# First frames' squares behind all their splits, first weights in two pieces, and the post-norm's g applied in the copy out of PSUM, in a two-layer streaming encoder

## The chip, the cores and the metric

The kernel runs on one core of one Trainium2 chip, as one launch. The metric is the device time of a launch in microseconds (us), the median of several runs. One launch of each kernel is also taken apart by the hardware profiler; its rows are what the text reads. TensorE is the matrix engine (PE in the rows, its weight loads PEld), VectorE is DVE, ScalarE is ACT, GpSimd is POOL, and SyncE (SP) issues all of the kernel's DMA transfers, in its own order. Matmul results land in PSUM, everything else lives in SBUF.

## The reference

Two layers run over 1056 frames of 1024 channels: 1024 frames of a new stream (the prompt) and 32 of a running one (the sample, with key and value caches). Each layer is a sandwich-normalised mixer:

```python
h = RMSNorm(x) * g_pre
au, av, az, bq, bk, bv, bz, cq, ck, cv, cz = split(h @ w_in)    # 1024 x 3072
ya = gMLP(au, norm(av)) * silu(az)           # mixing over chunks of 128 frames, 256 wide
yb = window_attention(bq, bk, bv, t5 bias, sinks) * silu(bz)    # own chunk of 64 + 2 before, 512 wide
yc = band_attention(cq, ck, cv, clipped bias) * silu(cz)        # own chunk + 8 before, 256 wide
y = concat(ya, yb, yc) @ w_out               # 1024 x 1024
x = x + RMSNorm(y) * g_post
```

The outputs are x of the prompt and the sample after the second layer, and the keys, values and normalised av rows that a later step would need. RMSNorm(y) is y times one number per frame, R = (mean of y squared + 1e-6) to the power -0.5; g is one number per channel.

## The kernel before

**Tiling.** Activations lie with channels on partitions: 8 k-chunks of 128 channels by 1056 frames. The frames form three tiles t0, t1, t2 of 384, 384 and 288 columns (the sample is the end of t2). `Y` holds the frames or the layer's values, `R` the factor per frame. Each operand of a dense matmul is split into a high and a low half: for activations `hh` and `hl` (with g_pre multiplied in), for weights `whi` and `wlo` (made from `wraw`, the tile as loaded, 128 x 512, four k-chunks). One k-step is three matmuls (hh by whi, hl by whi, hh by wlo). A dense block, 128 output channels by one frame tile, is 8 k-steps, so 24 matmuls, into one PSUM bank. A layer has 24 input blocks by 3 tiles (names bk bv bq0 ... cz1; letter a, b, c for the mixer) and 8 output blocks by 3 tiles. The weights of a few blocks are kept in the tiles named kk, vv, ph, pl rather than whi, wlo; the rows show these names.

**The norm before the matmul.** The first layer's blocks start before R is known, since R scales a whole frame: matmuls run on Y * g, and R is multiplied in when a block is copied out (`v<-S,R`, `v<-d,R`, `Y<-d,R`). R of a tile needs squares of its eight k-chunks (ScalarE), summed into a tile `v` (`v<-v,tmp`, VectorE or GpSimd), summed over partitions by TensorE (`pt<-ones,v`), turned into `r` (VectorE, then the power -0.5 on GpSimd with `mhalf`), and spread to all partitions by TensorE again (`pt<-ident,r`) and a ScalarE copy (`R<-pt`).

**What sets the order.** The program is written by a greedy planner while it is built. `Clock` (line 91) estimates when each engine is free. Work other than dense matmuls is put as steps into lanes (`lane(name).put(fn, ok, at, mark, ...)`): `ok` says which marks must be done, `at` when its operands are there. Before each k-step `pump` (line 1147) takes the steps that are ready. `two` (line 402) gives a two-input operation to VectorE or GpSimd, whichever ends it earlier by the estimate, and `copy` (line 415) picks ScalarE or VectorE. `split` (line 429) makes the high and the low half. So a change of one step shifts later choices all over the program. All instructions are recorded in one helper, which is why nearly all rows carry line L291; they are told apart by tile names.

**Buffers and tables.** PSUM has three banks named d, two named S (also used for scores), two pt and one pv. The order of the input blocks after the first three comes from the table `ORDERS`; the first three (bk, bv, bq0) run for t0 and t1 first, into d and S banks. SBUF tag "wraw" has 3 buffers, "v" 4, "tmp" 3.

**The places that the change touches.** `load`, `halve` and `split_at` (lines 499 to 540) load and split the weights. `square` (line 1203) does one chunk's square and its sum, and waits for the mark `0.X{t}.{k}`, chunk k's own split. `boundary` (line 1264) closes a layer for a tile: per chunk Y * g * R, plus the residual x, a store, and for the next layer the new split. The copy out of an output block is in the dense loop (line 1395); only the last tile of the last layer applies g there. `layer_consts` (line 1074) fills tables for the relative bias of mixer c.

Of the kernel before, what the change touches and what calls it, by code (L numbers as in the profile page):

```python
# [37 lines left out]
BLOCKS = "bk bv bq0 bq1 bq2 bq3 av0 av1 ck0 ck1 cv0 cv1 cq0 cq1 au0 au1 az0 az1 bz0 bz1 bz2 bz3 cz0 cz1".split()  # L38

ORDERS = (  # L40
    "bk bv bq0 bq2 bq1 bq3 av1 cq0 cv0 ck0 av0 bz2 cq1 cv1 au0 ck1 bz1 au1 az0 az1 bz3 bz0 cz1 cz0".split(),
    "bk bv bq0 bq1 bq2 av0 ck1 cv0 bq3 bz2 bz0 av1 ck0 cq0 cq1 bz1 cv1 au1 au0 bz3 az0 az1 cz0 cz1".split(),
)

FIRST = {"b": 0, "c": 4, "a": 6}
# [261 lines left out]
def encoder(  # L307
# [87 lines left out]
    def tmp():  # L395
        return tl([128, 384], "tmp")
# [46 lines left out]
    def lane(name):  # L443
        return lanes.setdefault(name, Lane())
# [42 lines left out]
    def take_spare(l, a="kk"):  # L487

        if l not in spare:
            x = tl([128, 2048], a, F32R)  # L490
            held[x.tensor.name] = 4
            spare[l] = [x[:, 512 * i : 512 * i + 512] for i in range(4)]

    for x in weights:
        kind, l, n = x[:3]
        for g in (0, 1):
            h = (x, g)

            def load(h=h, g=g, src=w[l, BLOCKS.index(n)] if kind == "w" else wo[l, n]):
                raw[h] = tl([128, 4, 128], "wraw")  # L500
                dma.dma_start(raw[h], src[:, 4 * g : 4 * g + 4, :])

            place = PLACES[2 * BLOCKS.index(n) + g] if kind == "w" and n in BLOCKS[:START] else None
            if kind == "o":
                place = KEPT.get((n, x[3]))

            def where(kind=kind, l=l, place=place, x=x):

                if kind == "o" and place:
                    return place if x in spare or {f"{l}.c1", f"{l}.SC"} <= done and free(place) else None  # L510
                if place == "kk":
                    return "kk" if l in spare or l == 0 or {f"{l - 1}.c1", f"{l - 1}.SC"} <= done and free("kk", 2) else None
                if place == "ph":
                    return "ph" if (l == 0 or f"{l - 1}.c1" in done) and free("ph") else None
                if free("whi"):
                    return "whi"
                return "ph" if kind == "o" and f"{l}.c1" in done and free("ph") else None

            def halve(h=h, l=l, n=n, kind=kind, where=where, x=x):
                a = where()  # L520
                if a in ("kk", "vv"):
                    to = l if kind == "w" else x
                    take_spare(to, a)
                    hi, lo = (spare[to].pop() for _ in (0, 1))
                else:
                    hi, lo = (tl([128, 512], c, F32R) for c in (a, {"whi": "wlo", "ph": "pl"}[a]))
                whi[h], wlo[h] = (x.rearrange("p (k c) -> p k c", k=4) for x in (hi, lo))
                split(whi[h], wlo[h], raw[h])
                let_go(raw.pop(h))

            def split_at(h=h, l=l, where=where, to=l if kind == "w" else x):
                a = where()
                t = after("act", [raw[h]])
                if a in ("kk", "vv"):
# [538 lines left out]

    def layer_consts(l):

        box = {}

        def mix():
            dma.dma_start(wt, aws[l])

            for g in range(4):
                pool.affine_select(wt[:, g, :], wt[:, g, :], pattern=[[1, 128]], compare_op=ALU.is_ge, fill=0.0,
                                   base=0, channel_multiplier=-1)

        def mix_bias(g):
            half = g % 2
            dma.dma_start(bsb[64 * half : 64 * half + 64, g // 2, :], abias[l, g : g + 1, :].to_broadcast([64, 128]))

        def sample_sink(j, g):
            dma.dma_start(ssk[32 * g : 32 * g + 32, j : j + 1],  # L1090
                          sinks[l : l + 1, 4 * j + g : 4 * j + g + 1].to_broadcast([32, 1]))
            if (j, g) == (1, 3):
                pool.tensor_scalar(ssk[:, 2:4], ssk[:, 0:2], -1.0, None, op0=ALU.mult)

        def table():
            c, e = box["c"], box["e"] = tmp(), tmp()
            dma.dma_start(c[:4, 0:256], crel[l, :, 1:257])
            pool.tensor_copy(c[:4, 256:384], c[:4, 255:256].to_broadcast([4, 128]))
            pool.tensor_copy(e[:4, :], c[:4, 255:256].to_broadcast([4, 384]))
            lane("store").put(lambda: dma.dma_start(fc_d[l][:, 0:384], c[:4, :]), None, lambda: after("dma", [c[:4, :]]))  # L1100
            lane("store").put(lambda: dma.dma_start(fc_d[l][:, 384:FC_W], e[:4, : FC_W - 384]), None,
                              lambda: after("dma", [e[:4, :]]), f"{l}.LC")

        return ([table, mix, lambda: dma.dma_start(gab, ag[l : l + 1, :].to_broadcast([128, 256]))]
                + [lambda g=g: mix_bias(g) for g in range(4)] + [lambda j=j, g=g: sample_sink(j, g) for j in (0, 1) for g in range(4)])

# [67 lines left out]
    def first_layer():  # L1174
# [20 lines left out]
        for t in range(3):  # L1195
            a, T = TOK[t]
            box = {}
            for k in range(KB):
# [6 lines left out]
                        box["sq"] = sq_tile(t)  # L1205
                    sq_add(box["sq"], Y[:, k, a : a + T], T, k == 0)

                lane(f"sq{t}").put(square, lambda k=k, ok=marks(f"0.X{t}.{k}"): ok() and (k or free("v")), lambda x_at=x_at: max(x_at(), clock.t["act"] - FIRST_AHEAD[3]), f"0.Q{t}.{k}")
            rms_steps(lane(f"bnd{t}"), box, t, marks(f"0.Q{t}.7"), f"0.R{t}")

    chunks = {}
# [55 lines left out]
    def boundary(l, t, box):  # L1267
# [7 lines left out]
        for k in range(8):  # L1275
            y = Y[:, k, a : a + T]

            def x(k=k, y=y):
                g = g_sb[:, l, 1, k : k + 1]
                dve.scalar_tensor_tensor(y, y, g, R[:, a : a + T], op0=ALU.mult, op1=ALU.mult)  # L1280
                c = chunk.pop(k)
                two(y, y, c[:, :T], ALU.add)
                let_go(c)
# [14 lines left out]
    def layer_steps(l):  # L1298
        units = [Unit(l, br, i, q) for br, n in (("b", 4), ("c", 2)) for i in range(n) for q in range(8 // NQ[br])]
        over = marks("0.R0") if l == 0 else marks(*(f"{l - 1}.{x}" for x in ("b3", "c1", "A", "SB", "SC")))  # L1300
        lane("lc").put(lambda: sink_consts(l), over, None, f"{l}.LS")
        for f in layer_consts(l):
            lane("lc").put(f, marks(f"{l}.b1.bias"), lambda: clock.t["dma"])
# [16 lines left out]
    for e, (x, t) in enumerate(plan):  # L1320
# [21 lines left out]
        for k in range(KB):  # L1342
            h = (x, k // 4)

            def at():
                if k == 0 and bank() is None or h not in whi or f"{l}.{'X' if kind == 'w' else 'ys'}{t}.{k}" not in done:
                    return None
                ops = [whi[h], wlo[h], hh[t][:, k, :], hl[t][:, k, :]]
                return max(after("pe", ops), slot(bank(), "pe") if k == 0 else 0.0)

            pump(at)
# [29 lines left out]
        else:  # L1381
# [123 lines left out]
```

## Time and profile before

| | us |
|---|---|
| median of three runs | 1014.42 |
| lowest, highest of them | 1014.22, 1015.7 |
| the profiled execution | 1014.88 |
| its span, first to last instruction | 1013.2 |
| TensorE, VectorE, ScalarE, GpSimd busy | 996.8, 762.9, 511.6, 69.5 |
| mean granted clock of TensorE | 0.998 |

The 1.7 us between the profiled execution's time and its span lie around the instructions. A busy share says how full an engine is; matmuls are pipelined, so a matmul's own duration (0.34 us at 384 columns) is about twice the distance from one start to the next in a full run. In a timeline a row shows its start, its duration, the engine and the operation with output and inputs, and in brackets the idle time before it and what ended that. The granted clock is 1.00 at full speed.

### The profile page before, as it was taken

How to read it: one execution, taken by the hardware profiler on the slowest of the kernel's cores; microseconds unless marked ns; L12 is line 12 of the kernel's file. 1: busy time of each engine (PE TensorE's matmuls, PEld its weight loads, DVE VectorE, ACT ScalarE, POOL GpSimd, SP SyncE). 2: the span in 40 equal slices, each digit the busy share in tenths (PEclk: the TensorE clock that was granted, in tenths of full speed). 3: DMA queues.
4: the chain of work that ended last, by engine and by line, in shares of the span. 5: the costliest groups of instructions: out<-in, count | busy, mean ns of one | idle time of the engine just before them, and what ended most of it. 6: DMA issues, size and time to landing. Idle time of an engine off the chain costs nothing.

```text
span 1013.2 us, 18902 instructions
## 1 busy us (share of the span) xinstructions
PE 996.8 (98%) x6630; PEld 969.2 (96%) x6630; DVE 762.9 (75%) x1973; ACT 511.6 (50%) x1304; POOL 69.5 (7%) x150
## 2 busy tenths in 40 slices
PE   8999999999999999999999999999999999999997
PEld 7999999989999999999999999999899999999996
DVE  8778778877777775858897789877687787577654
ACT  7555566554444443745643566645454444356332
POOL 0100000001100000000111000000200000000121
PEclk9999999999999999999999999999999999999999
DMA  8232313212123011446543322231122212126633
GB/s 267 68 79 79 84 50 88 64 48 57 58 66 96 22 43 63 145 126 187 153 137 114 79 66 78 59 85 35 52 67 64 65 43 75 42 76 196 188 109 128
DMA packets 83343, 91.26 MB, mean 90 GB/s; under 512 B 13232, under 2 KB 59696, under 8 KB 83248
## 3 DMA queue, kind: packets, MB, share of 16 engines
q1 hardware_dynamic: 83248, 90.05, 30.2%
q8 instruction: 52, 0.85, 0.4%
q14 instruction: 43, 0.35, 0.1%
HBM read 66.11 MB, written 11.31 MB: 76 GB/s over the span
## 4 chain that ended last, share of the span: by engine, by line
PE 82%; DVE 8%; DMA 3%; ACT 3%; issue 2%; SPq 1%; POOL 1%; DVEq 0%; ACTq 0%; POOLq 0%
PE d L291 54%; PE S L291 14%; PE pt L291 8%; PE pv L291 6%; DVE Y L291 3%; DVE s L291 1%; ACT tmp L291 1%; DVE wlo L291 1%; DVE pl L291 1%; DVE v L291 1%; SPq L291 1%; DMA wraw<-in_wo_dram 1%; DVE hl L291 1%; DMA wraw<-in_w_dram 1%; DMA bias<-fb_d 1%
## 5 line engine op out<-in xcount | busy, mean ns | idle before, releaser
L291 PE MATMUL d<-hh,whi 128*128 128x384 f32 (+1 forms) x1144 | 378.6, 331 | 0.0
L291 PE MATMUL d<-hh,wlo 128*128 128x384 f32 (+1 forms) x1144 | 369.7, 323 | 0.5 <-DVE wlo L291 0.4
L291 PE MATMUL d<-hl,whi 128*128 128x384 f32 (+1 forms) x1144 | 369.0, 323 | 0.0
L291 PEld LDWEIGHTS d<-hh,whi 128*128 128x128 f32 x1144 | 215.5, 188 | 2.2 <-issue 1.7
L291 PEld LDWEIGHTS d<-hh,wlo 128*128 128x128 f32 x1144 | 215.0, 188 | 1.3 <-DVE wlo L291 1.1
L291 PEld LDWEIGHTS d<-hl,whi 128*128 128x128 f32 x1144 | 215.7, 189 | 0.3
L291 ACT ACTIVATE s<-s,nm 128x256 f32<-128x256 f32 (+5 forms) x196 | 108.5, 554 | 150.0 <-DVE nm L291 149.8
L291 DVE TENSOR_TENSOR pl<-pt,ph 128x512 fp32r<-128x512 f32 (+2 forms) x136 | 80.6, 623 | 26.2 <-ACT ph L291 25.9
L291 DVE TENSOR_TENSOR wlo<-wraw,whi 128x512 fp32r<-128x512 f32 x116 | 80.2, 693 | 14.3 <-ACT whi L291 11.0
L291 ACT ACTIVATE ph<-pt 128x512 fp32r<-128x512 f32 (+2 forms) x136 | 69.0, 542 | 25.8 <-PE pt L291 24.7
L291 DVE TENSOR_TENSOR Y<-pv,tmp 64x256 f32<-64x256 f32 x96 | 40.4, 421 | 44.2 <-ACT tmp L291 43.2
L291 PE MATMUL pv<-pl,vv 128*128 128x256 f32 (+1 forms) x288 | 71.1, 286 | 0.6 <-DVE pl L291 0.3
L291 PE MATMUL pv<-ph,vv 128*128 128x256 f32 (+1 forms) x288 | 70.0, 269 | 0.2 <-ACT ph L291 0.2
L291 PE MATMUL pt<-ident,s 128*128 128x128 f32 x488 | 68.6, 274 | 0.0
L291 ACT ACTIVATE whi<-wraw 128x512 fp32r<-128x512 f32 x94 | 58.7, 624 | 18.5 <-DMA wraw<-in_wo_dram 13.7
L291 PE MATMUL S<-kk,qh 128*128 128x256 f32 (+3 forms) x224 | 66.1, 313 | 1.2 <-DVE nm L291 1.2
L291 PE MATMUL S<-kk,ql 128*128 128x256 f32 (+3 forms) x224 | 62.1, 295 | 0.0
L291 ACT ACTIVATE tmp<-tmp 128x384 f32<-128x384 f32 (+1 forms) x48 | 23.8, 496 | 68.1 <-DVE tmp L291 68.1
L291 PEld LDWEIGHTS pt<-ident,s 128*128 128x128 f32 x488 | 56.0, 140 | 2.2 <-DVE s L291 0.5
L291 PEld LDWEIGHTS pv<-pl,vv 128*128 128x128 f32 x288 | 54.4, 189 | 3.1 <-DVE pl L291 2.4
L291 DVE CUSTOM_DVE_ANT_0 s<-S,bias,nsink 128x256 f32<-128x256 f32 (+1 forms) x128 | 54.3, 463 | 2.8 <-POOL bias L291 1.5
L291 ACT ACTIVATE tmp<-pv 64x256 f32<-64x256 f32 x96 | 36.4, 379 | 39.2 <-DVE Y L291 20.4
(183 smaller groups left out, 1765.8 us busy)
## 6 DMA issues: line engine op xcount, KB each, us to landing
wraw<-in_w_dram SPq DMA_DIRECT2D x96, 256.0 KB, 2.9
wraw<-in_wo_dram SPq DMA_DIRECT2D x72, 256.0 KB, 3.0
qr<-Y SPq DMA_DIRECT2D x384, 32.0 KB, 1.9
x_d<-Y SPq DMA_DIRECT2D x16, 192.0 KB, 3.2
out_y_dram<-Y SPq DMA_DIRECT2D x16, 192.0 KB, 2.8
Y<-in_xT_dram SPq DMA_DIRECT2D x5, 576.0 KB, 4.8
bias<-fc_d SPq DMA_DIRECT2D x8, 320.0 KB, 3.8
bias<-fb_d SPq DMA_DIRECT2D x16, 128.0 KB, 3.1
```

The lines of the kernel that those rows point to most:

```text
L291: return f(*args, **kw)
```

## The change

Four edits. (1) The first weight tile is loaded in two transfers of 256 columns, and split in two pieces; a dense k-step may start with the first piece. (2) The `square` steps of t0 wait for the split of t0's last chunk, not of their own. (3) g of the post-norm is always applied in the copy out of PSUM; the boundary then multiplies by R only, by `two`, so on VectorE or GpSimd. The squares for the norm are still taken from PSUM, before g. (4) The two tables in `layer_consts` use tag "v" instead of "tmp". Beside them both tables `ORDERS` change: the first lines show one of them.

```diff
@@ ORDERS, one of its two lines
-    "bk bv bq0 bq2 bq1 bq3 av1 cq0 cv0 ck0 av0 bz2 cq1 cv1 au0 ck1 bz1 au1 az0 az1 bz3 bz0 cz1 cz0".split(),
+    "bk bv bq0 bq1 bq2 av1 bq3 cq0 cv0 ck0 av0 cq1 cv1 bz1 bz2 ck1 au1 az0 au0 az1 bz0 bz3 cz1 cz0".split(),
@@ -491,6 +491,15 @@
+    begin = (weights[0], 0)
+    ready = set()
+
+    def rest():
+
+        ready.add(begin)
+        split(whi[begin][:, 2:4, :], wlo[begin][:, 2:4, :], raw[begin][:, 2:4, :])
+        let_go(raw.pop(begin))
+
@@ -498,7 +507,9 @@
                 raw[h] = tl([128, 4, 128], "wraw")
-                dma.dma_start(raw[h], src[:, 4 * g : 4 * g + 4, :])
+                for k in (0, 2) if h == begin else (0,):
+                    m = 2 if h == begin else 4
+                    dma.dma_start(raw[h][:, k : k + m, :], src[:, 4 * g + k : 4 * g + k + m, :])
@@ -525,12 +536,17 @@
+                if h == begin:
+                    split(whi[h][:, 0:2, :], wlo[h][:, 0:2, :], raw[h][:, 0:2, :])
+                    lane("wsplit").steps.appendleft((rest, None, lambda: after("act", [raw[begin][:, 2:4, :]]), None, False, ()))
+                    return
+                ready.add(h)
                 split(whi[h], wlo[h], raw[h])
                 let_go(raw.pop(h))
...
@@ -1093,13 +1108,14 @@
-            c, e = box["c"], box["e"] = tmp(), tmp()
+            c, e = tl([128, 384], "v"), tl([128, 384], "v")
...
@@ -1205,7 +1221,7 @@
-                lane(f"sq{t}").put(square, lambda k=k, ok=marks(f"0.X{t}.{k}"): ok() and (k or free("v")), lambda x_at=x_at: max(x_at(), clock.t["act"] - FIRST_AHEAD[3]), f"0.Q{t}.{k}")
+                lane(f"sq{t}").put(square, lambda k=k, ok=marks(f"0.X{t}.{k if t else KB - 1}"): ok() and (k or free("v")), lambda x_at=x_at: max(x_at(), clock.t["act"] - FIRST_AHEAD[3]), f"0.Q{t}.{k}")
@@ -1277,7 +1293,7 @@
                 g = g_sb[:, l, 1, k : k + 1]
-                dve.scalar_tensor_tensor(y, y, g, R[:, a : a + T], op0=ALU.mult, op1=ALU.mult)
+                two(y, y, R[:, a : a + T], ALU.mult)
                 c = chunk.pop(k)
                 two(y, y, c[:, :T], ALU.add)
@@ -1343,9 +1359,9 @@
-                if k == 0 and bank() is None or h not in whi or f"{l}.{'X' if kind == 'w' else 'ys'}{t}.{k}" not in done:
+                if k == 0 and bank() is None or h not in whi or k % 4 > 1 and h not in ready or f"{l}.{'X' if kind == 'w' else 'ys'}{t}.{k}" not in done:
@@ -1392,7 +1408,7 @@
-            copy(Y[:, n, a : a + T], d[:, :T], g_sb[:, l, 1, n : n + 1] if end else None)
+            copy(Y[:, n, a : a + T], d[:, :T], g_sb[:, l, 1, n : n + 1])
```

The start of VectorE's program, as a piece of the difference between the two orders; hl_71 and hh_68 are the halves of t0, v_128 is the sum of its squares, wlo the weights' low halves (a row with x3 stands for three in a row):

```order
-L291 CAST whi_130<-wraw_93 128x512
-L291 TENSOR_TENSOR wlo_131<-wraw_93,whi_130 128x512
+L291 TENSOR_TENSOR wlo_130<-wraw_93,whi_129 128x256 x2
 L291 TENSOR_SCALAR hh_68<-Y,g_sb 128x384
-L291 SCALAR_TENSOR_TENSOR hl_71<-Y,g_sb,hh_68 128x384 x2
-L291 TENSOR_TENSOR v_128<-v_128,tmp_145 128x384
-L291 TENSOR_TENSOR v_128<-v_128,tmp_148 128x384
-L291 SCALAR_TENSOR_TENSOR hl_71<-Y,g_sb,hh_68 128x384 x2
-L291 TENSOR_TENSOR wlo_162<-wraw_97,whi_161 128x512
-L291 TENSOR_TENSOR v_128<-v_128,tmp_165 128x384
-L291 TENSOR_TENSOR v_128<-v_128,tmp_168 128x384
+L291 SCALAR_TENSOR_TENSOR hl_71<-Y,g_sb,hh_68 128x384 x4
```

Four square sums stood between the low halves of t0; now four low halves follow one another, and the first weight's high half is no longer made on VectorE.

Later on VectorE, before the first copy out of a block (S_141 before, S_138 now: block bk of t0). Before:

```order
L291 SCALAR_TENSOR_TENSOR hl_72<-Y,g_sb,hh_69 128x384 x3
L291 TENSOR_TENSOR v_259<-v_259,tmp_292 128x384
L291 SCALAR_TENSOR_TENSOR hl_73<-Y,g_sb,hh_70 128x288
L291 TENSOR_TENSOR v_259<-v_259,tmp_300 128x384
L291 TENSOR_TENSOR v_259<-v_259,tmp_306 128x384
L291 TENSOR_TENSOR v_259<-v_259,tmp_312 128x384
L291 SCALAR_TENSOR_TENSOR hl_73<-Y,g_sb,hh_70 128x288
L291 TENSOR_TENSOR v_325<-S_141,R 128x384
L291 CAST kk_124<-v_325 64x384
```

And after, where v_192 sums the squares of t0, v_327 those of t1, v_385 those of t2, and r_364 is r of t0:

```order
L291 TENSOR_TENSOR v_192<-v_192,tmp_324 128x384
L291 TENSOR_TENSOR v_327<-v_327,tmp_332 128x384
L291 TENSOR_TENSOR v_327<-v_327,tmp_338 128x384
L291 TENSOR_TENSOR v_327<-v_327,tmp_344 128x384
L291 TENSOR_TENSOR v_327<-v_327,tmp_357 128x384
L291 TENSOR_SCALAR r_364<-pt_360 128x3
L291 TENSOR_TENSOR v_327<-v_327,tmp_367 128x384
L291 TENSOR_TENSOR v_327<-v_327,tmp_373 128x384
L291 TENSOR_TENSOR v_327<-v_327,tmp_379 128x384
L291 TENSOR_TENSOR v_385<-v_385,tmp_391 128x288
L291 TENSOR_TENSOR v_385<-v_385,tmp_394 128x288
L291 TENSOR_TENSOR v_405<-S_138,R 128x384
```

The last sum of t0 and the r made from it now stand behind all the low halves of t0, t1 and t2 (hl_73), and the copy out behind the sums of two tiles.

The boundary of tile t1 in the last layer, on VectorE. Before:

```order
L291 SCALAR_TENSOR_TENSOR Y<-Y,g_sb,R 128x384
L291 TENSOR_TENSOR Y<-Y,s_12223 128x384
L291 SCALAR_TENSOR_TENSOR Y<-Y,g_sb,R 128x384
L291 TENSOR_TENSOR Y<-Y,s_12234 128x384
L291 SCALAR_TENSOR_TENSOR Y<-Y,g_sb,R 128x384
L291 TENSOR_TENSOR Y<-Y,bias_12249 128x384
L291 SCALAR_TENSOR_TENSOR Y<-Y,g_sb,R 128x384
L291 TENSOR_TENSOR Y<-Y,bias_12269 128x384
L291 SCALAR_TENSOR_TENSOR Y<-Y,g_sb,R 128x384
L291 TENSOR_TENSOR Y<-Y,bias_12285 128x384
L291 TENSOR_TENSOR wlo_12581<-wraw_12367,whi_12580 128x512
L291 TENSOR_TENSOR v_12475<-v_12475,tmp_12618 128x288
```

After, on VectorE:

```order
L291 TENSOR_TENSOR Y<-Y,R 128x384
L291 TENSOR_TENSOR Y<-Y,s_12182 128x384
L291 TENSOR_TENSOR Y<-Y,s_12193 128x384
L291 TENSOR_TENSOR Y<-Y,s_12217 128x384
L291 TENSOR_TENSOR Y<-Y,s_12226 128x384
L291 TENSOR_TENSOR Y<-Y,s_12237 128x384
L291 TENSOR_TENSOR Y<-Y,R 128x384
L291 TENSOR_TENSOR Y<-Y,bias_12246 128x384
L291 TENSOR_TENSOR Y<-Y,bias_12266 128x384
L291 TENSOR_TENSOR Y<-Y,R 128x384
L291 TENSOR_TENSOR Y<-Y,bias_12281 128x384
L291 TENSOR_TENSOR wlo_12583<-wraw_12370,whi_12582 128x512
```

And after, on GpSimd, where before no Y row stood:

```order
L291 TENSOR_TENSOR r_12463<-r_12463,mhalf 128x3
L291 MEMSET v_12478 128x96
L291 TENSOR_TENSOR Y<-Y,R 128x384 x4
L291 TENSOR_TENSOR v_12478<-v_12478,tmp_12525 128x288
L291 TENSOR_TENSOR Y<-Y,R 128x384
L291 TENSOR_TENSOR pl_12556<-wraw_12358,ph_12555 128x512
L291 TENSOR_TENSOR v_12478<-v_12478,tmp_12573 128x288
```

Three of the eight multiplies by R stay on VectorE and five stand on GpSimd, among the square sums of t2 and a weight's low half (pl).

VectorE in the second layer, around a copy out (v from d) and the first scores of mixer b (ISA rows: scores plus bias). Before:

```order
L291 SCALAR_TENSOR_TENSOR Y<-Y,g_sb,R 128x288
L291 TENSOR_TENSOR Y<-Y,bias_6523 128x288
L291 TENSOR_TENSOR ql_6809<-qr_6728,qh_6808 128x256
L291 ISA s_6812,nm_6813<-S_6815,bias_6784,nsink 128x128
L291 ISA nm_6813 128x1
L291 ISA s_6812,nm_6813<-S_6815,bias_6784,nsink 128x128
L291 ISA nm_6813 128x1
L291 TENSOR_TENSOR v_6827<-d_6762,R 128x384
L291 TENSOR_SCALAR hh_70<-Y,g_sb 128x288
```

After:

```order
L291 TENSOR_TENSOR Y<-Y,R 128x288
L291 TENSOR_TENSOR Y<-Y,bias_6525 128x288
L291 TENSOR_TENSOR ql_6806<-qr_6734,qh_6805 128x256
L291 TENSOR_TENSOR ql_6822<-qr_6739,qh_6821 128x256
L291 TENSOR_TENSOR v_6829<-d_6795,R 128x384
L291 SCALAR_TENSOR_TENSOR hl_73<-Y,g_sb,hh_70 128x288
L291 TENSOR_TENSOR v_6636<-v_6636,tmp_6833 128x288
L291 ISA s_6847,nm_6848<-S_6850,bias_6758,nsink 128x128
L291 ISA nm_6848 128x1
```

The copy out of d stood behind the score rows, and now stands ahead of them.

## Rows read from the trace of the kernel before

**Rows 1.** The page's first part: busy us, share of the span, instructions.
```profile
PE 996.8 (98%) x6630; PEld 969.2 (96%) x6630; DVE 762.9 (75%) x1973; ACT 511.6 (50%) x1304; POOL 69.5 (7%) x150
```
**Rows 2.** TensorE's waits, two of 16: us in total, times, longest.
```profile
PE pt L291 <- POOL mhalf L291: 1.4, 1, 1.4
...
PE pt L291 <- DVE r L291: 0.8, 1, 0.8
```
**Rows 3.** Stretches of the start: length, PE busy (matmuls), clock, DMA share, GB/s.
```profile
12.64:16.11 3.47, 3.47 (x13) 0.51 0.83 252
16.11:19.62 3.51, 3.51 (x22) 1.00 1.02 339
```
**Rows 4.** Timeline of TensorE, start: start, duration, operation, idle before.
```profile
12.36 0.46 PE L291 MATMUL S<-hl,whi 128*128 128x384 f32 x1 [1.04 <-DVE hl L291]
```
**Rows 5.** Timeline of VectorE at the start.
```profile
5.29 0.69 DVE L291 TENSOR_TENSOR wlo<-wraw,whi 128x512 fp32r<-128x512 f32 x1
6.24 0.42 DVE L291 TENSOR_SCALAR hh<-Y,g_sb 128x384 fp32r<-128x384 f32 x1 [0.26 <-DMA Y<-in_xT_dram]
6.70 1.15 DVE L291 SCALAR_TENSOR_TENSOR hl<-Y,g_sb,hh 128x384 fp32r<-128x384 f32 x2
7.76 1.22 DVE L291 TENSOR_TENSOR v<-v,tmp 128x384 f32<-128x384 f32 x2
...
11.69 1.67 DVE L291 SCALAR_TENSOR_TENSOR hl<-Y,g_sb,hh 128x384 fp32r<-128x384 f32 x3
```
**Rows 6.** Timeline of SyncE's issues at the start.
```profile
1.72 0.42 SPq L291 DMA_DIRECT2D wraw<-in_w_dram  x1
...
6.39 0.64 SPq L291 DMA_DIRECT2D Y<-in_xT_dram  x1
```
**Rows 7.** Timeline of TensorE, a return to dense matmuls and the sixth block's start.
```profile
29.95 0.42 PE L291 MATMUL d<-hh,whi 128*128 128x384 f32 x1
30.22 0.34 PE L291 MATMUL d<-hl,whi 128*128 128x384 f32 x1
...
35.44 0.34 PE L291 MATMUL S<-hh,kk 128*128 128x384 f32 x1
```
**Rows 8.** Timeline of ScalarE: R of t0.
```profile
24.80 0.49 ACT L291 ACTIVATE R<-pt 128x384 f32<-128x384 f32 x1 [1.20 <-PE pt L291]
```
**Rows 9.** Timeline of GpSimd: the power for r of t0.
```profile
20.71 1.08 POOL L291 TENSOR_TENSOR r<-r,mhalf 128x3 f32<-128x3 f32 x1 [19.26 <-DVE r L291]
```
**Rows 10.** Timeline of SyncE: loads of the first q pieces.
```profile
33.48 5.00 SPq L291 DMA_DIRECT2D qr<-Y  x8
```
**Rows 11.** Timeline of TensorE: two waits, second layer's scores and last boundary.
```profile
536.29 0.55 PE L291 MATMUL pt<-ident,v 128*128 128x128 f32 x3 [0.91 <-DVE v L291]
...
990.99 0.41 PE L291 MATMUL S<-hh,wlo 128*128 128x288 f32 x1 [0.80 <-DVE wlo L291]
```
**Rows 12.** Timeline of VectorE: a score instruction of the second layer.
```profile
535.01 0.35 DVE L291 CUSTOM_DVE_ANT_0 s<-S,bias,nsink 128x128 f32<-128x128 f32 x1 [1.52 <-POOL bias L291]
```
**Rows 13.** Groups of ScalarE: count, busy us and mean ns, idle before.
```profile
L291 ACT ACTIVATE Y<-d,g_sb 128x288 f32<-128x288 f32 x5 | 2.5, 496 | 0.0
...
L291 ACT ACTIVATE Y<-d 128x288 f32<-128x288 f32 x5 | 2.0, 404 | 0.0
```
**Rows 14.** Group of VectorE: the boundary's multiply at 384 columns.
```profile
L291 DVE SCALAR_TENSOR_TENSOR Y<-Y,g_sb,R 128x384 f32<-128x384 f32 x32 | 23.6, 739 | 11.5 <-ACT R L291 11.5
```
**Rows 15.** Timeline of VectorE in t1's boundary, last layer.
```profile
978.75 0.56 DVE L291 TENSOR_TENSOR Y<-Y,s 128x384 f32<-128x384 f32 x1
...
980.99 1.09 DVE L291 TENSOR_TENSOR Y<-Y,s 128x384 f32<-128x384 f32 x1
```
**Rows 16.** Timeline of GpSimd in the same stretch.
```profile
980.85 0.80 POOL L291 TENSOR_TENSOR v<-v,tmp 128x288 f32<-128x288 f32 x1 [4.83 <-ACT tmp L291]
```
**Rows 17.** Groups of GpSimd at 384 columns.
```profile
L291 POOL TENSOR_TENSOR hl<-Y,hh 128x384 fp32r<-128x384 f32 x4 | 4.1, 1020 | 129.0 <-ACT hh L291 129.0
L291 POOL TENSOR_TENSOR v<-v,tmp 128x384 f32<-128x384 f32 x3 | 3.8, 1259 | 18.8 <-ACT tmp L291 18.8
```

More of the change, by code (lines that the diff above doesn't have):

```diff
@@ L40 @@
 ORDERS = (
-    "bk bv bq0 bq2 bq1 bq3 av1 cq0 cv0 ck0 av0 bz2 cq1 cv1 au0 ck1 bz1 au1 az0 az1 bz3 bz0 cz1 cz0".split(),
-    "bk bv bq0 bq1 bq2 av0 ck1 cv0 bq3 bz2 bz0 av1 ck0 cq0 cq1 bz1 cv1 au1 au0 bz3 az0 az1 cz0 cz1".split(),
+    "bk bv bq0 bq1 bq2 av1 bq3 cq0 cv0 ck0 av0 cq1 cv1 bz1 bz2 ck1 au1 az0 au0 az1 bz0 bz3 cz1 cz0".split(),
+    "bk bv bq0 bq1 bq2 ck1 bq3 cv0 bz0 av0 av1 bz2 ck0 cq0 cq1 bz1 cv1 bz3 au1 au0 az1 cz0 cz1 az0".split(),
 )
@@ L532, in split_at @@
                 a = where()
-                t = after("act", [raw[h]])
+                t = after("act", [raw[h][:, 0 : 2 if h == begin else 4, :]])
                 if a in ("kk", "vv"):
@@ L1074, in layer_consts @@
     def layer_consts(l):
-        box = {}
         def mix():
@@ L1099, in table @@
             pool.tensor_copy(e[:4, :], c[:4, 255:256].to_broadcast([4, 384]))
-            lane("store").put(lambda: dma.dma_start(fc_d[l][:, 0:384], c[:4, :]), None, lambda: after("dma", [c[:4, :]]))
-            lane("store").put(lambda: dma.dma_start(fc_d[l][:, 384:FC_W], e[:4, : FC_W - 384]), None,
-                              lambda: after("dma", [e[:4, :]]), f"{l}.LC")
+            store(fc_d[l][:, 0:384], c[:4, :], c)
+            store(fc_d[l][:, 384:FC_W], e[:4, : FC_W - 384], e)
+            lane("store").put(lambda: None, None, None, f"{l}.LC")
+            let_go(c, e)
         return ([table, mix, lambda: dma.dma_start(gab, ag[l : l + 1, :].to_broadcast([128, 256]))]
@@ L1301, in layer_steps @@
         lane("lc").put(lambda: sink_consts(l), over, None, f"{l}.LS")
-        for f in layer_consts(l):
-            lane("lc").put(f, marks(f"{l}.b1.bias"), lambda: clock.t["dma"])
+        for i, f in enumerate(layer_consts(l)):
+            lane("lc").put(f, lambda i=i: f"{l}.b1.bias" in done and (i or free("v", 2)), lambda: clock.t["dma"])
         lane("lc").put(lambda: None, None, None, f"{l}.LD")
@@ L1345, in at @@
             def at():
-                if k == 0 and bank() is None or h not in whi or f"{l}.{'X' if kind == 'w' else 'ys'}{t}.{k}" not in done:
+                if k == 0 and bank() is None or h not in whi or k % 4 > 1 and h not in ready or f"{l}.{'X' if kind == 'w' else 'ys'}{t}.{k}" not in done:
                     return None
-                ops = [whi[h], wlo[h], hh[t][:, k, :], hl[t][:, k, :]]
+                ops = [whi[h][:, k % 4, :], wlo[h][:, k % 4, :], hh[t][:, k, :], hl[t][:, k, :]]
                 return max(after("pe", ops), slot(bank(), "pe") if k == 0 else 0.0)
```

## The prediction, as made before the changed kernel ran

> **What bounds the kernel now.** I read the busy shares first: TensorE works 98% of the 1013.2 us span, VectorE 75%, ScalarE 50%, GpSimd 7% [rows 1]. So time comes back only where TensorE stands idle, runs at the slow clock, or is interrupted. Next the list of what it waited for: no entry is over 1.4 us, and the longest, for GpSimd's mhalf, is outside the change; an entry of 0.8 for r is inside it [rows 2]. Then the start by stretches: from 12.64 to 16.11 us TensorE's granted clock is 0.51, the lower of its two levels (1.2 GHz), and after that 1.00 [rows 3]. Timelines of the start, of the scores in the second layer and of the last boundary give what an instruction takes and waits.
>
> **The start: squares behind splits, first weight in two pieces.** At 12.36 TensorE starts the low-half matmul of frames' k-chunk 5, after 1.04 us of waiting for hl [rows 4]. VectorE, which makes that half, runs without a gap from 6.24 on, and ahead of the group of three hl at 11.69 it does two pairs of square sums; the pair at 7.76 takes 1.22 us, with a little overlap into the next, and the other is like it [rows 5]. The change moves those four sums behind, and gives VectorE one hh cast that ScalarE made before (0.42 by the row at 6.24 [rows 5]). Replayed from 6.24 with the durations of these rows less the overlap of neighbours: hh to 6.7, four hl at 0.55 to 8.9, a wlo to 9.5, then hh and hl of chunk 5. Their input is the frames' load of chunks 5 to 7, whose issue SyncE ends at 7.03 [rows 6]; I estimate its landing somewhat under 10 us, so the half is there at 10.7 to 11.0. Against 12.36 that is 1.3 us earlier.
>
> With it the slow stretch should go, for it sets in behind that long wait: 13 matmul rows in 3.47 us there, 22 in 3.51 after it [rows 3], which is nine matmuls fewer at 0.16, or 1.4 us. It may also stay, since other pauses of TensorE lie ahead of it; rival (a) has that price. Wait and clock together give 2.7. The low halves that come next (two wlo, one pl of the third block's weights) then follow VectorE closely, and I estimate 0.4 back for them: the first three blocks end 2.3 us earlier.
>
> The two-piece load costs SyncE one more issue ahead of all later frame loads, 0.42 us by the issue of the first weight [rows 6], and brings the first subtraction forward by at most half of its 0.69 [rows 5]. Bounds for the first matmul -0.3 and +0.5. I take 0, since chunk 5 decides later anyway. A rule of the Trainium skill speaks against the two pieces: "DMA: Bandwidth & Descriptors", section "Measured (HBM→SBUF, 128 partitions, SWDGE, issued from GpSimd)", asks for large transfers and shows far less bandwidth at 64 KB than at 1 MB. No half of a weight is loaded in the run of before, so no row shows it for these sizes; by the rule the gain of the first piece would vanish, which the 0 above already grants.
>
> What is late next is R of the first tile, because its squares now come last. The sixth block needs a bank that only a copy out frees, and the copy needs R. Before, R was built at 24.80 and the sixth block began at 35.44 [rows 7, 8], over 10 us of slack. After, the first copy out stands behind ten square sums in a row. Replayed down VectorE's new order (eight hl of tile 1 and eight of tile 2 ahead of them), r comes at 28.5, GpSimd's power takes 1.08 [rows 9], R is there near 31 after one more trip over TensorE, the copy out ends near 31.9, and the sixth block starts then. Before, it started at 35.44 behind some 0.9 us of small transposes that now come later, so 34.5 for equal work: -2.6. Queued behind are SyncE's loads of the q pieces, 5.00 us from 33.48 on [rows 10], which feed the first scores; they move with R and the copies, at worst 1 us into the gain. **Start: -2.5**, bounds -3.3 (nothing eaten) and 0 (R two to three us later than replayed).
>
> **The new block orders.** Counted in the two orders of TensorE, the matmuls are the same, and returns to a dense pass after other work fall from 257 to 247. A return costs 0.27 from its first matmul's start to the next (29.95 to 30.22 [rows 7]) against 0.16 in a full run [rows 3]: 0.1 us each, **-1.0**. Of the waits, 0.91 for v at 536.29 [rows 11] comes from a copy out that stands on VectorE behind a score instruction, which waits 1.52 us for its bias at 535.01 [rows 12]. In the new order that copy stands ahead of the scores: **-0.9**. New waits of this kind may arise where other blocks now meet the attention; the longest of before is 1.4, so I allow two either way, -2 to +2 around zero.
>
> **g in the copy out.** Forty more of ScalarE's copies take g: 0.496 with it and 0.404 without at 288 columns [rows 13], 40 x 0.09 = 3.7 us on an engine that is 50% busy [rows 1]. The copy frees a bank, but blocks turn over three of them, so it hides behind the next block's matmuls: 0. If that cover failed, all 3.7 would show.
>
> **The multiply at the boundary.** VectorE loses forty multiplies (32 of them at 0.739 in the mean [rows 14]); in the new order GpSimd takes 27 and VectorE 13. What a GpSimd one costs its neighbour shows in the last boundary: beside the 0.80 us sum of GpSimd at 980.85, VectorE's sum of 980.99 takes 1.09, against 0.56 for the same at 978.75 [rows 15, 16]. VectorE is held for about GpSimd's time less 0.3. The Trainium skill says why in "SBUF — State Buffer", section "Who interferes with whom": a VectorE instruction with two SBUF inputs contends with a GpSimd one that reads SBUF. The trace agrees in these rows.
>
> For 384 columns on GpSimd the nearer row is 1.02 [rows 17]: 0.7 held for some 0.6 saved, +0.1 an instruction, so five in the boundary of tile 1 of the last layer give +0.5. Three on VectorE are 0.05 shorter each, and a weight subtraction there that held VectorE from GpSimd goes back to it: together near **0** for the end of its chain, and so for the 0.80 wait for wlo behind it at 990.99 [rows 11]. Bounds: were nothing held, 3 us earlier, worth at most that 0.80 and the 0.8 for r; were all serial, five x 0.41 = 2 us later in each of two such places. For all boundaries I take 0, range -1.6 to +4.
>
> The tables of c and e take other buffers with the same stores, and their lane waits for two free ones, far from need: nothing.
>
> **Sum.** -2.5 - 1.0 - 0.9 + 0 = -4.4 against the profiled execution's 1014.88: **1010.5 us**. That execution lies between the lowest and the highest of the three runs, 0.46 over their median, so I leave it.
>
> **Rivals.**
> (a) The start's gain is eaten: R of tile 0 comes two us and more later than replayed, or the slow stretch stays. For it: ten sums on a VectorE that has no gap there, then GpSimd's power and two trips over TensorE in series. Against it: slack of 10 us before. Time: 1014.88 - 1.9, with 0.5 back for the extra issue, 1013.5, no change.
> (b) Slower: GpSimd holds VectorE at the boundaries. The place is VectorE's chain of multiply, sum and then wlo or r, for which TensorE already waits [rows 2, 11]. It decides once that chain ends over 1 us later, which it does at 1.26 a multiply, as GpSimd's 384-column sum takes [rows 17]: held 0.96 to 1.26 for 0.61, 27 times, is 9.5 to 17.6 us of VectorE time over the boundaries. If half reaches TensorE, 4.7 to 8.8, less the 4.4: 1015.2 to 1019.3; I take 1017.5. Against it: VectorE is 75% busy, and most of the boundary has blocks of TensorE work beside it.
> (c) A larger gain: the waits for r and wlo go as well (1.6), and the boundaries give their best elsewhere (another 1.5): 1007.4. For it: VectorE sheds some 20 us.
> That the change doesn't do what it says is out for g, whose multiplies are gone from the order; for the start it is (a).
>
> **Numbers.** My forecast (1008.5 to 1012.4) has 0.52, (c) 0.17, (a) 0.20, (b) 0.11. The 80% range takes most of (c), all of (a) and the low end of (b): 1006.8 to 1015.0. A measurement of this kernel tells about 0.2%, 2 us, from no change: faster is under 1012.4, which holds the forecast, (c) and a little of (a), 0.71; within 2 us 0.19; slower 0.10.
>
> **What will show it.** Right: chunk 5's low-half matmul near 11 us with at most 0.3 of waiting; no stretch at half clock before 20 us; the sixth block near 32; no 0.9 wait for v beside the second layer's first scores; the last layer's wlo behind tile 1's boundary as long after its R as before. Wrong: TensorE waiting for r, R or a bank before the sixth block; a wait over 1.5 us for wlo or r behind a boundary, with GpSimd multiplies of 1.2 us and more beside it.

## The result, and the profile after

The changed kernel takes 1031.36 us (median of 4 runs, 1029.67 to 1032.26) against 1015.06 for the kernel before (4 runs); the ratio is 1.0151, 95% interval 1.0137 to 1.0166. It is slower by some 16 us, where 4.4 less were forecast, and lies outside the range. The profiled execution has a span of 1029.9 us.

The busy shares hardly tell it (to be held against [rows 1]): GpSimd does 41 us more, VectorE 5 us more, and TensorE, at 8 us more, is still at 98%.

```profile
PE 1005.0 (98%) x6630; PEld 974.7 (95%) x6630; DVE 767.6 (75%) x1947; ACT 510.7 (50%) x1295; POOL 110.7 (11%) x187
```

TensorE's waits (us in total, times, longest) show a new first entry. The last line is the boundary wait for wlo that the prediction watched, now 0.4 for the 0.8 of [rows 11].

```profile
PE pt L291 <- DVE v L291: 6.6, 3, 3.9
PE d L291 <- DVE wlo L291: 1.7, 2, 1.6
PE S L291 <- DVE ql L291: 1.6, 1, 1.6
...
PE S L291 <- DVE wlo L291: 0.4, 1, 0.4
```

**The start went as forecast.** In the two stretches of [rows 3], the first now has 22 matmul rows at full clock for 13 at half:

```profile
12.64:16.11 3.47, 3.47 (x22) 1.00 0.97 307
16.11:19.62 3.51, 3.48 (x20) 1.00 1.02 355
```

Part of this contrast is chance. x6 below runs the program of before without a change up to the first layer's output blocks. TensorE waits there at 12.24 for the same 1.04 us, and yet runs at full clock in the same stretch:

```profile
12.64:16.11 3.47, 3.47 (x22) 1.00 0.76 249
```

On the timeline of TensorE, chunk 5's low half starts at 11.24 without a wait [rows 4], and the sixth block at 32.57 [rows 7]:

```profile
11.24 0.45 PE L291 MATMUL S<-hl,whi 128*128 128x384 f32 x1
...
32.57 0.45 PE L291 MATMUL S<-hh,kk 128*128 128x384 f32 x1
```

r of tile 0 (VectorE), its R (ScalarE, [rows 8]) and the q loads (SyncE, [rows 10]), from three timelines, come late, as replayed:

```profile
28.94 0.15 DVE L291 TENSOR_SCALAR r<-pt 128x3 f32<-128x3 f32 x1
```
```profile
31.43 0.49 ACT L291 ACTIVATE R<-pt 128x384 f32<-128x384 f32 x1 [0.60 <-PE pt L291]
```
```profile
38.96 5.16 SPq L291 DMA_DIRECT2D qr<-Y  x8
```

**The loss sits between the layers.** I counted the dense matmuls in each trace and took the start of the n-th. The first 144 (six blocks) are the same work in every kernel here; further on the orders mix other work between, so a few us of difference in the middle are no loss.

| n-th dense matmul starts at (us) | before | after | x1 (no g) | x5 (norm later) | x12 (multiplies out) | x9 (start alone) |
|---|---|---|---|---|---|---|
| 144 | 41.35 | 38.63 | 39.11 | 38.66 | 38.96 | 39.25 |
| 240 | 58.79 | 56.50 | 57.12 | 57.58 | 56.88 | 63.90 |
| 801 | 196.00 | 196.01 | 196.85 | 196.35 | 196.03 | 200.98 |
| 2001 | 458.65 | 457.86 | 458.44 | 457.91 | 457.78 | 463.81 |
| 2201 | 492.50 | 499.07 | 492.29 | 492.31 | 491.64 | 497.66 |
| 2501 | 546.83 | 562.93 | 546.68 | 553.65 | 546.87 | 552.29 |

The lead is 2.7 us at the sixth block, none at 196 us and 0.8 just ahead of the boundaries (matmul 2001 of the layer's 2304). Single executions differ by more than that 0.8: at matmul 2001, the six with the new start, the new orders and the planner's own price for GpSimd stand at 457.8 to 458.6, mean 458.1, and the three with the old start and the old orders at 456.8 to 458.7, mean 457.9. So no lead of the start is left there. Then 7.4 us go in the boundary of tile 0 (from 2001 to 2201) and 9.5 in that of tile 1 (to 2501). Stretches of 4 us there, first of before and then of after (stretch, length, PE busy (matmuls), clock, DMA share, GB/s):

```profile
468.00:472.00 4.00, 4.00 (x25) 1.00 0.67 198
472.00:476.00 4.00, 4.00 (x25) 1.00 0.88 269
476.00:480.00 4.00, 4.00 (x30) 1.00 0.46 130
```
```profile
468.00:472.00 4.00, 2.73 (x16) 1.00 0.78 210
472.00:476.00 4.00, 1.33 (x7) 0.83 0.98 328
476.00:480.00 4.00, 4.00 (x14) 0.50 0.50 183
...
520.00:524.00 4.00, 4.00 (x15) 0.50 0.61 189
```

TensorE stands first, and then runs at its lower level. The instruction that waits is the sum over partitions of tile 0's squares for the next norm. In before two such sums stand close together. The one at 479.71 belongs to tile 1's post-norm. Tile 0's is the one at 481.18, since VectorE adds the last of its squares from 480.32 to 480.87. It stands behind the 2130th dense matmul. In after it stands behind the 2073rd, that of 470.39, which is 57 matmuls or ten and a half us earlier in TensorE's queue, and its data come only just before 474.67 (timelines of VectorE and TensorE of before, then of TensorE of after):

```profile
480.32 0.55 DVE L291 TENSOR_TENSOR v<-v,tmp 128x384 f32<-128x384 f32 x1
```
```profile
479.71 0.73 PE L291 MATMUL pt<-ones,v 128*128 128x1 f32 x6
...
481.18 0.72 PE L291 MATMUL pt<-ones,v 128*128 128x1 f32 x6
```
```profile
470.39 0.34 PE L291 MATMUL d<-hh,vv 128*128 128x384 f32 x1
474.67 1.41 PE L291 MATMUL pt<-ones,v 128*128 128x1 f32 x6 [3.95 <-DVE v L291]
```

So the sum is ready some six us earlier than in before; it is only asked for still earlier. VectorE and GpSimd in that boundary of after (two timelines):

```profile
449.35 1.25 DVE L291 TENSOR_TENSOR Y<-Y,s 128x384 f32<-128x384 f32 x1
450.71 0.98 DVE L291 TENSOR_SCALAR hh<-Y,g_sb 128x384 fp32r<-128x384 f32 x1
```
```profile
448.80 1.39 POOL L291 TENSOR_TENSOR Y<-Y,R 128x384 f32<-128x384 f32 x1 [2.31 <-ACT R L291]
450.27 1.21 POOL L291 TENSOR_TENSOR Y<-Y,s 128x384 f32<-128x384 f32 x1
451.44 4.82 POOL L291 TENSOR_TENSOR Y<-Y,R 128x384 f32<-128x384 f32 x4
```

VectorE's sum takes 1.25 for 0.56 [rows 15] and the cast of hh 0.98 for 0.42 [rows 5], while GpSimd works back to back. In the groups by shape (count, busy us, mean ns, idle before) the multiply takes 1.31 us on GpSimd and 0.74 in the mean on VectorE:

```profile
L291 POOL TENSOR_TENSOR Y<-Y,R 128x384 f32<-128x384 f32 x22 | 28.3, 1308 | 8.9 <-ACT R L291 8.9
```
```profile
L291 DVE TENSOR_TENSOR Y<-Y,R 128x384 f32<-128x384 f32 x10 | 7.4, 744 | 12.7 <-ACT R L291 12.7
```

### The profile page after: what moved, and what is told of

It is laid out like the page before. It is cut to its first block, busy times and chain, and to the rows that moved or that the text cites. A ratio compares the mean times of both kernels' runs of the same rounds, so it can differ in the third digit from the quotient of the medians.

```text
span 1029.9 us, 18891 instructions
## 1 busy us (share of the span) xinstructions
PE 1005.0 (98%) x6630; PEld 974.7 (95%) x6630; DVE 767.6 (75%) x1947; ACT 510.7 (50%) x1295; POOL 110.7 (11%) x187
## 4 chain that ended last, share of the span: by engine, by line
PE 70%; DVE 14%; ACT 5%; DMA 4%; issue 3%; SPq 3%; POOL 0%; DVEq 0%; ACTq 0%; POOLq 0%
PE d L291 47%; PE S L291 10%; PE pt L291 8%; PE pv L291 5%; DVE Y L291 4%; SPq L291 3%; DVE hl L291 2%; DVE v L291 2%; DVE s L291 2%; ACT tmp L291 1%; DVE pl L291 1%; DMA wraw<-in_wo_dram 1%; DMA qr<-Y 1%; DVE wlo L291 1%; ACT s L291 1%
## 5 line engine op out<-in xcount | busy, mean ns | idle before, releaser
L291 DVE TENSOR_TENSOR wlo<-wraw,whi 128x512 fp32r<-128x512 f32 (+1 forms) x115 | 79.1, 690 | 11.8 <-ACT whi L291 8.6
L291 ACT ACTIVATE whi<-wraw 128x512 fp32r<-128x512 f32 (+1 forms) x93 | 57.2, 619 | 16.0 <-DMA wraw<-in_wo_dram 9.0
L291 DVE TENSOR_TENSOR v<-v,tmp 128x384 f32<-128x384 f32 (+1 forms) x76 | 44.0, 583 | 24.3 <-ACT tmp L291 23.0
```

Of the source, the lines that this page charges most:

```text
L291: return f(*args, **kw)
```

## The experiments

The first theory, G, was that GpSimd's multiplies cost the time by holding VectorE; the rival, O, that the new order does. From the fifth run on the theory was P: the planner, once it may give the multiply to GpSimd, places later steps too early in TensorE's queue. Ratios are to the kernel before on the same chip, with 95% intervals.

**x1_without_g.** The g edit undone in the changed kernel:

```diff
-                two(y, y, R[:, a : a + T], ALU.mult)
+                dve.scalar_tensor_tensor(y, y, g, R[:, a : a + T], op0=ALU.mult, op1=ALU.mult)
...
-            copy(Y[:, n, a : a + T], d[:, :T], g_sb[:, l, 1, n : n + 1])
+            copy(Y[:, n, a : a + T], d[:, :T], g_sb[:, l, 1, n : n + 1] if end else None)
```

> The changed kernel with the g edit undone: the copy out of PSUM carries no g, and the boundary multiplies by g and R on VectorE again; the start, the block orders and the tables stay as changed. The planner writes the order anew behind the first layer's blocks; up to there it is that of the changed kernel. Theory G (GpSimd's multiplies at the boundaries hold VectorE, TensorE then waits and its clock drops): the loss of some 16 us goes, and the start's 2 us stay: 1009 to 1014. Rival O (the new block orders cost it): 1024 or more. Rival S (squares late at the start): over 1018.

Measured 1017.32, ratio 1.0023 (1.0013 to 1.0032), against 1014.94. That is outside G's range, but some 14 us come with the g edit as planned. The other three together still lose 2.4, where 4.4 less was forecast; up to matmul 2501 they lose nothing (546.68 for 546.83), and the loss is in the rest of the second layer. Tile 0's sum for the next norm stands behind the 2130th dense matmul again, at 480.96.

**x2_same_order_vector.** The order kept, the multiplies issued to VectorE:

```diff
+        e = (dve, pool)[min(ends)[1]]
+        if to is not None:
+            clock.run(e.key, "tensor_tensor", [out], [a, b])
+            to.real.tensor_tensor(out, a, b, op)
+            return
...
-                two(y, y, R[:, a : a + T], ALU.mult)
+                two(y, y, R[:, a : a + T], ALU.mult, to=dve)
```

> The changed kernel with the planner's order kept instruction for instruction, but every multiply by R of a boundary is issued to VectorE at its place, none to GpSimd; the boundary's sums that stand on GpSimd stay there. Theory G: the waits of TensorE at the end of the layer 0 boundaries (3.95 and 2.01 for v, 1.55 for a weight's low half) shrink to under half and so do the stretches at half clock: 1012 to 1020. Rival O: the order of the other instructions sets these waits, the engine of the multiply does not matter: 1027 to 1033.

Measured 1036.76, ratio 1.0211 (1.0196 to 1.0227): slower still, and outside both ranges. With VectorE doing all multiplies, the sum is later (timeline of TensorE):

```profile
475.68 1.41 PE L291 MATMUL pt<-ones,v 128*128 128x1 f32 x6 [4.78 <-DVE v L291]
```

G as it was put falls: in this order GpSimd is the better engine for these multiplies, by 5 us.

**x3_orders_alone.** Before, with the two new tables `ORDERS` (their lines as in the change).

> The kernel before with the two new block orders and nothing else. Theory G: within 4 us of before, 1010 to 1018. Rival O: 1022 or more. The term of the prediction for the orders was -1.9: 1012.5.

Measured 1029.9, ratio 1.0147 (1.0132 to 1.0162). A miss for G, but not the loss of the changed kernel: the boundaries between the layers are clean (33.85 us from matmul 2001 to 2201, as before), and the loss lies in the first layer and in the middle of the second. Its longest waits are for weights (first rows of the list):

```profile
PE d L291 <- DVE whi L291: 3.6, 4, 1.8
PE d L291 <- ACT whi L291: 2.4, 2, 1.4
PE S L291 <- DVE kk L291: 2.3, 1, 2.3
```

Weights are issued behind long trains of q pieces in SyncE's queue (timeline). That these trains make the loss is argued, not shown: before has two of 16 as well, from 77.83 and 163.73, and no run moved them.

```profile
100.13 13.99 SPq L291 DMA_DIRECT2D qr<-Y  x16
114.22 1.00 SPq L291 DMA_DIRECT2D bias<-fb_d  x2
115.33 1.87 SPq L291 DMA_DIRECT2D wraw<-in_w_dram  x2
```

**x4_before_order_gpsimd.** Before's order, with 25 multiplies on GpSimd:

```diff
-                dve.scalar_tensor_tensor(y, y, g, R[:, a : a + T], op0=ALU.mult, op1=ALU.mult)
+                r = R[:, a : a + T]
+                clock.run("dve", "scalar_tensor_tensor", [y], [y, g, r])
+                (pool if k in (1, 2, 3, 4, 6) else dve).real.tensor_tensor(y, y, r, ALU.mult)
```

> The kernel before in its own order, instruction for instruction, with g in the copy out and five of the eight multiplies by R of each of the five planned boundaries (chunks 1, 2, 3, 4 and 6) issued to GpSimd instead of VectorE, 25 in all. Theory G: each holds VectorE 0.7 to 1.0 us for the 0.6 it saves, and two boundaries in a layer's end run into TensorE's waits: 1018 to 1030. Rival O: the multiply's engine costs nothing: 1013 to 1016.

Measured 1015.83, ratio 1.0006 (0.9996 to 1.0016): no change. Such multiplies cost nothing where TensorE asks for tile 0's sum at its old place, behind the 2130th dense matmul (timeline of TensorE):

```profile
480.92 0.74 PE L291 MATMUL pt<-ones,v 128*128 128x1 f32 x6
```

**x5_norm_4us_later.** One step later in TensorE's queue:

```diff
-            rms_steps(ln, nb, t, None, f"{l + 1}.R{t}")
+            rms_steps(ln, nb, t, None, f"{l + 1}.R{t}", 4000.0)
...
-        ln.put(one, ok, lambda: max(after("pe", [box[x] for x in ("sq", "more") if x in box]), slot("pt", "pe")), pe=True)
+        ln.put(one, ok, lambda: max(after("pe", [box[x] for x in ("sq", "more") if x in box]) + late, slot("pt", "pe")), pe=True)
```

> The changed kernel, but the step that sums the next layer's squares over partitions on TensorE (pt from ones and v) at the two boundaries after layer 0 is held back by 4 us in the planner's reckoning, so that its matmuls stand some 4 us later in TensorE's queue; up to the first of them the program is the changed kernel's. Theory P (TensorE's queue holds that step earlier than VectorE, slowed beside GpSimd, can have the sum ready; the wait of 3.95 and the one of 2.0, and the half clock behind each, are the loss): the waits for v fall under 1 us each, no half clock between 470 and 530 us, 1016 to 1022. Rival O (other instructions' places in the new order cost it): the waits move to the weights' low halves or to R, 1027 to 1032.

Measured 1023.1, ratio 1.007 (1.0055 to 1.0085): 8.3 us less than the changed kernel, just outside what was expected. The sum of tile 0 now stands behind the 2094th dense matmul, 21 later than in after. In tile 0's boundary wait and half clock are gone (TensorE's timeline, then a stretch of 10 us, where the changed kernel had 6.05 us busy at 0.73):

```profile
474.71 0.80 PE L291 MATMUL pt<-ones,v 128*128 128x1 f32 x6 [0.29 <-DVE v L291]
```
```profile
470.00:480.00 10.00, 9.71 (x62) 1.00 0.77 252
```

At tile 1 P's forecast failed. Its boundary still has waits (hh 2.1, wlo 1.5, v 1.3) and a clock of 0.67 from 512 to 516, and by the table 7.0 of its 9.5 us stay, so 4 us for the norm's step alone do not mend it.

**x6_before_order_g.** Before's order, g in the copy, R alone on VectorE. The diff is x4's with `dve` in place of the choice of engine.

> The kernel before in its own order, instruction for instruction, with g in the copy out of PSUM and the boundary's multiply by R alone on VectorE at its old place. The g edit without any new plan: theory P and the prediction's sum for ScalarE (nothing) and 40 multiplies of 0.56 for 0.61 on VectorE say no change, 1013 to 1016. If ScalarE's longer copies do cost, up to 1018.

Measured 1014.19 against 1015.37, ratio 0.9986 (0.9977 to 0.9995): a little faster, and the fastest complete version here. The trace doesn't place that gain at the edit. At matmul 144, where the program is still that of before, this execution is 1.5 us ahead already (39.82 for 41.35), as it has no slow stretch behind the wait at 12.24; at matmul 2501 it is 1.5 ahead, and at the last dense matmul 0.8.

**x7_orders_tables.** x3 with the tables c and e in tag "v".

> The kernel before with the new block orders and the tables of the relative bias in the other buffers, nothing else: the orders alone gave 1029.9, with tables and the start edits 1017.3. If the tables' buffers make the new orders bearable: 1016 to 1021. If the start edits do: 1027 to 1032. In both cases theory P expects no wait over 1.5 us for v behind the boundaries.

Measured 1029.1, ratio 1.0132 (1.0117 to 1.0147), with the waits of x3 (whi 4.2 together, kk 2.3). The tables do not help; it is with the start edits that the new orders do not lose there.

**x8_gpsimd_cost.** One number of the planner:

```diff
-        return 140.0 + 2.25 * n
+        return 140.0 + 2.9 * n
```

> The changed kernel with one number of the planner's reckoning changed: a two-input instruction of GpSimd costs 0.14 us and 2.9 ns a column, 1.25 us at 384 columns as the trace of the changed kernel has it (1.13 to 1.39), where it was 2.25 ns and 1.00 us. The planner writes a new order from the first layer on. Theory P: with a truer price the sums are not asked for too early, the waits for v at the boundaries shrink to under half of 6.6: 1014 to 1022, more if the new plan of the first layer is poor. Rival O: 1027 and more, with the waits where they were.

Measured 1039.96, ratio 1.023 (1.021 to 1.025). Time and waits both miss what P expected, and the time lies in O's range. It is no clean test of either, as the whole plan changed and 8 us are lost by matmul 2001. Tile 0's sum stands only 15 dense matmuls later than in after and still waits 3.2 us for v, with tile 1's 4.6 in all. One truer price does not make the plan true.

**x9_start_alone.** The start edits, and from the 73rd pass through `pump` the steps in the order in which before took them (`replay` reads them from a list, and skips what is done):

```diff
+        seen[0] += 1
+        if seen[0] > SWITCH:
+            replay()
+            return
```

> The kernel before with its own block orders and only the start edits: the first weight in two pieces, and the squares of tile 0 behind all its splits. The planner writes the first nine blocks; from there on the steps are taken in the order that the kernel before had (a list of them stands in the program), so beyond the first layer's third block of rows the orders of all engines are those of before. The prediction's start term by itself: -2.5, so 1011.8 to 1013.3 where nothing eats it. Rival (the lead, 2.7 us at the sixth block of the changed kernel, is lost to the first layer's scores and weights later): 1014 to 1015.5.

Measured 1020.99, ratio 1.0052 (1.0034 to 1.007), slower than both ranges. The lead of 2.1 at the sixth block becomes a lag of 5.1 at matmul 240. TensorE waits twice for q of early scores, and its clock falls. The longer wait is for a q load, since VectorE stood idle for the transfer ahead of its cast to qh (timelines of TensorE and VectorE; the stretch):

```profile
51.75 0.39 PE L326 MATMUL S<-kk,qh 128*128 128x256 f32 x1 [0.99 <-DVE qh L326]
...
54.63 0.58 PE L326 MATMUL S<-kk,qh 128*128 128x256 f32 x1 [1.80 <-DVE qh L326]
```
```profile
54.29 0.29 DVE L326 CAST qh<-qr 128x256 fp32r<-128x256 f32 x1 [2.13 <-DMA qr<-Y]
```
```profile
50.00:60.00 10.00, 7.14 (x31) 0.67 0.33 80
```

**x10_start_and_g.** x9 with the edit of x6.

> The start edits as in the run on the start alone, and with them g in the copy out of PSUM and the boundary's multiply by R alone on VectorE, both without a new plan: the orders of before stay. If the two gains (2.5 predicted for the start, 1.2 measured for g in the old order) add: 1010.5 to 1012.5, faster than both kernels. If the start gives nothing: 1013.5 to 1014.5.

Measured 1019.75, ratio 1.0048 (1.003 to 1.0066): outside both ranges. It is 1.2 less than x9, but the two intervals overlap, and so do the single runs, so it isn't shown that a gain of the g edit adds. The start's gain does not exist in this order.

**x11_all_edits_old_reckoning.** x1 with the edits of x4: all four edits, planned as if g and R were multiplied on VectorE.

> All edits of the changed kernel with its block orders, start and tables, but the planner reckons as if g and R were still multiplied on VectorE at the boundary: g goes into the copies, and chunks 1, 2, 3, 4 and 6 of each boundary are multiplied by R on GpSimd (25 of them, 27 in the changed kernel), at places that were chosen without knowing it. Theory P (what the planner makes of the edit costs the 14 us, not the instructions): within 3 of the run without g, 1015.5 to 1020. Rival G (GpSimd's multiplies hold VectorE, at 1.31 us each in the changed kernel): 1025 or more.

Measured 1018.93, ratio 1.0034 (1.0023 to 1.0045). P holds: TensorE's order is x1's, with tile 0's sum behind the 2130th dense matmul, and 25 multiplies on GpSimd are 1.6 us over x1 (1.1 by the ratios), where the changed kernel is 14 over it with 27.

**x12_multiplies_left_out.** x2 with nothing issued where the planner had chosen GpSimd.

> The changed kernel in its own order, with the 27 multiplies by R that stand on GpSimd left out (those chunks are not normalised); nothing takes their place, and the rest of every engine's order is the changed kernel's. Theory P (TensorE's queue asks for sums that VectorE's chain, held beside GpSimd, has ready 4 us too late): without the multiplies the chain is ahead of its place in the queue, the 3.95 wait goes and so do most of the others behind the boundaries: 1013 to 1019. Rival O (the waits come from something else in the order): 1026 or more.

Measured 1014.99, ratio 1.0002 (0.9992 to 1.0012). In an order equal to the changed kernel's on TensorE and VectorE, 16 us are gone with these 27. VectorE ends the sum at 470.24, and TensorE takes it without a wait; the hh cast is back at 0.42 (timelines of TensorE and VectorE):

```profile
470.48 0.72 PE L291 MATMUL pt<-ones,v 128*128 128x1 f32 x6
```
```profile
450.44 0.42 DVE L291 TENSOR_SCALAR hh<-Y,g_sb 128x384 fp32r<-128x384 f32 x1
...
469.22 1.02 DVE L291 TENSOR_TENSOR v<-v,tmp 128x384 f32<-128x384 f32 x2
```

## Why the prediction was wrong

**The step that failed is the boundary's multiply: "together near 0 for the end of its chain"**, with bounds that let it cost TensorE at most 4 us. It measured 14 (after against x1) to 16 (after against x12). I priced how much later VectorE's chain ends against the place where TensorE asked for it before, and I priced it in the last layer. There it held: TensorE's wait for wlo is 0.4 for 0.8, and from matmul 2501 to the last the changed kernel loses 0.7. I carried it over to all boundaries, but those of layer 0 go on with the next layer's split, its squares and the norm's sum, and the new order moves that sum: tile 0's went ten and a half us forward in TensorE's queue, and it showed in the program before any run. Where the sum keeps its old place (x4, x11), 25 such multiplies cost up to 2 us, so the near 0 was about right for the instructions, and wrong for the plan. That the 27 multiplies are what makes VectorE late for that queue is shown by x12, and by x2 that they do so on either engine; that the place in the queue turns it into lost time is shown by x5 for tile 0. For tile 1 only x12 speaks: without the multiplies its boundary takes 55.2 us (matmul 2201 to 2501) for 63.9, and 54.3 in before. Its waits for hh, wlo and v were not taken apart one by one.

The size inside that step was off as well. I took 1.02 for a GpSimd multiply of 384 columns; it takes 1.31, and it holds the hh cast too, 0.98 for 0.42. The Trainium skill has the second in "SBUF — State Buffer", section "Who interferes with whom": tensor_scalar can enter a mode with two ports, and can then contend with GpSimd. The trace agrees here, as the cast is back at 0.42 in x12, and I had applied the rule to two-input instructions only.

**The clock was priced at the start and forgotten at the boundary.** Behind the 3.95 wait, 14 matmul rows run in 4 us where before has 25 to 30, and the wait of 2.01 for v at tile 1 (518 us) is followed by such a stretch too, from 520 on. A wait of 4 us so cost 7.4.

**The start, "-2.5", was about right where it was worked out** (r 28.94, R 31.43, sixth block 32.57, forecast 28.5, 31, 31.9). The first dense matmul came at 4.77 for 5.31, half a us earlier, where the two pieces were put at 0 (-0.3 to +0.5). The end of the sixth block varies from run to run: in the nine profiled executions with the new start its last matmul starts at 38.6 to 39.7 us, mean 39.1, in the five with the old one at 39.8 to 42.1, mean 41.2, so the lead is 2.1. As a term of the sum it was wrong: nothing of it is left at matmul 2001. The step that failed was "they move with R and the copies, at worst 1 us into the gain" for SyncE's q loads: in the old order 7 us are lost at early scores, with TensorE waiting for q (x9); with the new block orders the lead fades in the attention that follows, and what eats it there is not shown.

**The block orders, "-1.0" and "-0.9"**, were counted apart from the rest. Ten returns fewer are true of the changed kernel. Its 0.9 wait for v is gone too, but not by the orders: with them and without the g edit such a wait stays, 1.1 in x1, 0.6 in x3, 0.9 in x7; and beside the same scores the changed kernel has a new wait of 1.6 for ql, at 547.18. With the old start these orders lose 14 (x3, x7), with the new one 2.4 together with it (x1). So neither has a term of its own that could be added.

**g in the copy: nothing on ScalarE** was right: x6 is no slower than before. VectorE's multiply takes 0.72 there for 0.74 at 384 columns and 0.45 for 0.51 at 288, 1.0 us over all forty; that the 1.2 by which x6 is faster comes from these was not shown, and its lead at matmul 144 speaks against it.

Rival (b) named the right place, VectorE's chain behind the multiply, but not the cause. GpSimd holds VectorE, as it said, and yet with the multiplies on VectorE it is slower still (x2); and its point of decision (the chain ending over 1 us later than before) was not what happened: the chain ends earlier than before, and later than the new queue wants it.

What stays open: what in the planner's reckoning puts the sum so early (a truer price for GpSimd did not mend it, x8), why the new orders lose so much with the old start, and which of the three waits at tile 1 comes first.

## What to carry to other kernels

When an order is written by a planner, a new choice of engine changes what the planner believes, and each in-order queue is then filled to that belief: compare where the waiting engine's instruction stands before and after, not only how long the chain before it takes. An edit can be tested apart from its plan by reckoning the old instruction and issuing the new one; here that separates instructions that cost up to 2 us (x4, x6, x11) from a plan that loses 14. A lead is worth only what the next in-order queue (in x9 SyncE's loads of q) can follow.

## What the runs showed of the hardware

A GpSimd multiply of 128 x 384 takes 1.31 us (22 of them). Beside GpSimd's work a cast with one input more than doubles, 0.98 for 0.42 (after against x12). After a wait of 3.95 us that ended at 474.67, TensorE's granted clock was 0.50 from 476 to 480, and with waits of 0.99 and 1.80 us within 4 us it was 0.67 over 10 us (x9). A wait of 1.04 us at the same place of the same program was followed by 0.51 over 3.5 us in one execution (before) and by 1.00 in another (x6).
